# An attention block in split fp32: GpSimd's share of the weight splits in pieces of 256 columns, output weights loaded ahead of y, first key and query tiles in the norm's buffers

## The chip, the cores and the metric

The kernel runs on one core of a Trainium2 chip. The metric is device time in microseconds (us) of one execution, taken as the median of several. The engines are named as the profile names them: PE (TensorE, matrix products and transposes; PEld is its weight load), DVE (VectorE), ACT (ScalarE), POOL (GpSimd) and SP (SyncE, which here issues nearly all DMAs).

## The reference

One layer of a streaming encoder on 1024 tokens of width 1024, all in fp32:

```python
n = rms_norm(h, norm1_g)
qa, ka, va, qb, kb, vb = split(n @ w_in)          # 512,128,128 | 512,512,512 columns
ya = mixer_a(qa, ka, va, sinks)      # window of 3 chunks of 64, 8 heads on 2 key heads, ALiBi, sinks
yb = mixer_b(qb, kb, vb, rel_bias)   # own chunk + 8 before it, 8 heads, relative bias
y = concat(rms_norm(ya, og_a), rms_norm(yb, og_b))
h = h + y @ w_out
u = square(relu(rms_norm(h, norm2_g) @ w_ff1))    # 1024 -> 4096
h = h + u @ w_ff2                                 # 4096 -> 1024
return rms_norm(h, final_norm_g)
```

## The kernel before

**Arithmetic.** Each fp32 operand of a product is held as two rounded parts: hi = round(a) and lo = a - hi. A product is then three matmuls (`mm3`, line 154: hi·hi, hi·lo, lo·hi). So every tile that goes into PE costs an ACT copy (hi, rounded on the way out) and a subtraction (lo). The subtraction is `split_l` (line 133, instruction at L134); the caller says on which engine it runs, DVE or POOL.

**Weights.** `load_weight` (from line 160) takes a staging tile (tag "ws", 3 buffers), loads one weight into it (L110, on SP's queue), has ACT copy hi into one page (L171) and `low_engine` subtract lo into another. A weight of the input projection is a tile of 128 partitions by 8 blocks of 128 columns (1024 columns); a weight of the output projection (`out_weight`) is 128x1024, done in two halves of 512. For the first key and query weights `low_engine` is DVE; for all others here it is POOL. The weights of the MLP have a split of their own that the change does not touch.

**Projection.** `project` computes 512 tokens of 128 projected columns in one PSUM tile. `place` takes it out: DVE multiplies by the tokens' scale R (L242 for q, L244 for k) into a tile `ts_...` (tag "tst", 2 buffers), ACT copies hi, POOL or DVE subtracts lo, and DMAs of SP spread the parts over the K and Q tiles that the attention reads (L251 for Q, L254 for K). A v tile is kept and transposed on PE later (`turn_v`, VA and VvB in the profile). The "tst" buffer is free again when those DMAs have landed.

**Stages.** (1) Start: x and its transpose are loaded; kA, qA0 and vA are projected for both halves t of the tokens (`first_place`), and the norm's scales are computed. The tiles of x wait in "xs" (6 buffers of the pool `sp`, released as a whole before the attention begins). (2) Mixers A and B, 42 to about 407 us: units of attention (scores S, exponentials P, normalisation L494 or L559, transposes pt, products av), interleaved on PE with "filler" work: the other input projections (qA1 to qA3, then kB, qB, vB four times) and the first half of the output projection (`out_proj_a`: weights o0 to o3, and the rows y of mixer A, which had been written to DRAM as yd and are loaded again by `load_y`, L633). (3) The second half of the output projection, the MLP in a form with seven products instead of eight, and the last norm.

**What sets the order.** Each engine works its instructions off in order. PE's order is written out by hand: with `pe_order` on, each PE instruction depends on the one before. The other engines' orders come from a scheduler, which goes by the order in the source and by dependencies. `load` (from line 108) adds a dependency on the marked load before it (`last_load`), which keeps SP's loads behind that one. All DMAs of SP go through one queue in the order of SP; an issue that has to wait holds back all behind it. Both kernels have the same PE instructions in the same order.

Of the kernel before, what the change touches and what calls it, by code (L numbers as in the profile page):

```python
# [9 lines left out]
F32R = mybir.dt.float32r  # L10
# [5 lines left out]
P = 128  # L16
# [4 lines left out]
HALF = 512  # L21
DFF = 4096
NQ = DFF // (4 * P)
HD = 64
# [2 lines left out]
BIG = 3e38  # L27
QA0, KA0, VA0, QB0, KB0, VB0 = 0, 512, 640, 768, 1280, 1792
NPAGES = 35
GQ = 2  # L30
AHEAD1 = 2
AT_ONCE = 3
# [12 lines left out]
def kernel(  # L45
# [34 lines left out]
    def f(ap):  # L80
        return ap.bitcast(F32)
# [51 lines left out]
    def split_l(engine, lo, full, hi):  # L133
        engine.tensor_tensor(lo, full, f(hi), ALU.subtract)  # L134
# [25 lines left out]
    def load_weight(src, shape, name, low_engine, cuts=1, pieces=1):  # L160

        st = stage(shape, f"st_{name}")
        w = [page(shape, f"w{hl}_{name}") for hl in range(2)]

        def steps():
            n = shape[1] // cuts
            for i in range(0, shape[1], n):
                load(st[:, i : i + n], src[:, i : i + n])
                for j in range(i, i + n, n // pieces):
                    c = slice(j, j + n // pieces)  # L170
                    nc.scalar.activation(w[0][:, c], st[:, c], AF.Copy)  # L171
                    split_l(low_engine, w[1][:, c], st[:, c], w[0][:, c])
                yield

        if cuts > 1:
            return w, steps()
        for _ in steps():
            pass
        return w
# [18 lines left out]
    xs = {}  # L198
# [30 lines left out]
            n = [nT[t][hl][k // 2][:, k % 2, :] for hl in range(2)]  # L229
            mm3(acc, (w[0][:, k], w[1][:, k]), n, k == 0, k == NK - 1)  # L230

    def place(acc, kind, name, dst, t, low_engine):
        if name == "vA":
            st = page([P, 2, HALF], f"ts_{name}_{t}")
        else:
            st = main.tile([P, 2, HALF], F32R, tag="tst", bufs=2, name=f"ts_{name}_{t}")
        c = slice(t * HALF, (t + 1) * HALF)
        if kind == "v":
            nc.vector.tensor_tensor(f(st[:, 0]), acc, R1[:, c], ALU.mult)
            return lambda *where: turn_v(st, name, dst, t, *where)  # L240
        if kind[0] == "q":
            nc.vector.scalar_tensor_tensor(f(st[:, 1]), acc, HD**-0.5, R1[:, c], ALU.mult, ALU.mult)  # L242
        else:
            nc.vector.tensor_tensor(f(st[:, 1]), acc, R1[:, c], ALU.mult)  # L244
        nc.scalar.activation(st[:, 0], f(st[:, 1]), AF.Copy)
        split_l(low_engine, st[:, 1], f(st[:, 1]), st[:, 0])
        for hl in range(2):
            for s in range(2):
                src = f(st[s * HD : (s + 1) * HD, hl])
                if kind == "q":  # L250
                    nc.sync.dma_start(f(dst[s][hl * HD : (hl + 1) * HD, c]), src)  # L251
                else:
                    for rep in range(2):
                        nc.sync.dma_start(f(dst[2 * hl + s][rep * HD : (rep + 1) * HD, c]), src)  # L254

    def turn_v(st, name, dst, t, psum, tag, bufs):
        tp = psum.tile([P, 4, 2, HD], F32, tag=tag, bufs=bufs, name=f"vt_{name}_{t}")
# [19 lines left out]
    def in_proj(c0, kind, name, dst, new):  # L277

        w = proj_weight(c0, name, nc.gpsimd)
        yield  # L280
        later = None
        for t in range(2):
            acc = aps.tile([P, HALF], F32, tag="w", bufs=3, name=f"ip_{name}_{t}")
            for k in range(NK):
                project(acc, w, t, (k,))
                if k == 2 and later:
                    later(aps, "w", 3)
                if k == NK - 1:
                    if t == 0:
                        dst.extend(new(name))  # L290
                    later = place(acc, kind, name, dst, t, nc.gpsimd)
                yield
        if later:
            yield
            yield
            later(aps, "w", 3)
# [26 lines left out]

    def first_place(n, t, acc):
        kind, _, name, dst = first[n]
        return place(acc, kind, name, dst, t, nc.vector)

    accs = [first_acc(n, 0) for n in range(3)]
    for n, ks in [(n, (k, k + 1)) for k in range(0, NK, 2) for n in range(2)] + [(2, range(NK))]:
# [7 lines left out]
    Qs = [Q, [], [], []]  # L337
    ahead_A1 = in_proj(QA0 + P, "q", "qA1", Qs[1], new_q)
    next(ahead_A1)
    project(accs[2], wts[2], 1, (0, 1))  # L340
    turns[2](sps, "r", 2)
    project(accs[2], wts[2], 1, (2, 3))
# [287 lines left out]
    def load_y(m):  # L630
        y = new_y(m)
        for t in range(2):
            nc.sync.dma_start(f(y[t]), yd[m, :, t])  # L633
        return y
# [57 lines left out]
    def out_proj_a():  # L692
        ys, ws = [], []
        for m in range(4):
            ys.append(load_y(m))
            ws.append(out_weight(m))
        yield
        for tb in range(TB):
            h = hres[tb] = page([P, D], f"h{tb}", F32)
            nc.sync.dma_start(h, x[tb * P : (tb + 1) * P, :])  # L700
            for dh in range(2):
                c = slice(dh * HALF, (dh + 1) * HALF)
                ps = aps.tile([P, HALF], F32, tag="w", bufs=3, name=f"op_A_{tb}_{dh}")
                for q in range(4):
                    out_proj_step(ps, ys, ws, q, tb, c)
                    if q == 3:
                        nc.vector.scalar_tensor_tensor(h[:, c], ps, rA[:, tb : tb + 1], h[:, c], ALU.mult, ALU.add)  # L707
                    yield
# [537 lines left out]
```

## Time and profile before

| quantity | value |
|---|---|
| runs | 1086.87, 1089.08, 1090.6 us; median 1089.08 |
| profiled execution | 1091.92 us, of it 1090.1 us span (1.8 outside) |
| PE busy in the span | 1056.1 us, 97% |
| DVE, ACT, POOL busy | 759.1 (70%), 535.8 (49%), 426.1 (39%) us |
| mean granted PE clock | 0.994 |
| DMA share of the queue q1 | 47.2% |

A row of the timeline reads: start, duration, engine, line, operation, output <- inputs, shape, count, and in square brackets how long the engine stood idle before it and what released it; where a row holds several instructions, its duration is from the first's start to the last's end. The chain of waits gives per pair of waiting and releasing instruction the total, the count and the longest. A window gives each engine's busy time in a stretch, then the granted PE clock (1.00 is full), the DMA share and the traffic.

### The profile page before, as it was taken

The page shows a single profiled execution, that of the slowest core. Times are in us where ns is not written, and L with a number is a line of the kernel's source. Part 1 is how long each engine was busy: PE and PEld are TensorE (multiplying, and loading weights), DVE is VectorE, ACT ScalarE, POOL GpSimd, SP SyncE. Part 2 cuts the span into 40 slices and gives each one's busy share as a digit, 9 for nine tenths or more (in the row PEclk, how much of TensorE's full clock was granted, in tenths as well). Part 3 has the DMA queues.
Part 4 walks back from the last instruction along what each step waited for, and adds up shares of the span by engine and source line. Part 5 has one row for each costly group of instructions (what it writes and reads, how often), then busy time and mean ns, then how long its engine had stood idle before and what let it go on. Part 6 is the DMA issues. An engine that isn't in the chain of part 4 may idle for free.

```text
span 1090.1 us, 14323 instructions
## 1 busy us (share of the span) xinstructions
PE 1056.1 (97%) x5040; PEld 876.2 (80%) x5040; DVE 759.1 (70%) x1162; ACT 535.8 (49%) x953; POOL 426.1 (39%) x256
## 2 busy tenths in 40 slices
PE   8998999999999999998999999999999999999997
PEld 6787877888878888876888888888788888888885
DVE  5576788757667665597756555655988776778667
ACT  7676766656565466655333333334423333333346
POOL 1364665333252142347644453464014124024125
PEclk9999999999999999998999999999999999999999
DMA  9944626343566432122445255326898545532004
GB/s 332 246 124 120 163 79 170 99 120 113 134 211 239 136 126 107 78 96 95 176 160 188 97 174 174 138 94 248 286 394 316 164 136 173 175 116 97 1 1 155
DMA packets 90584, 170.30 MB, mean 156 GB/s; under 512 B 7824, under 2 KB 43664, under 8 KB 90512
## 3 DMA queue, kind: packets, MB, share of 16 engines
q1 hardware_dynamic: 90368, 169.38, 47.2%
q8 instruction: 40, 0.66, 0.3%
q14 instruction: 32, 0.26, 0.1%
q10 hardware_dynamic: 144, 0.00, 0.0%
HBM read 105.39 MB, written 45.09 MB: 138 GB/s over the span
## 4 chain that ended last, share of the span: by engine, by line
PE 82%; DVE 8%; DMA 3%; ACT 3%; issue 2%; SPq 1%; POOL 1%; DVEq 0%; ACTq 0%
PE f L128 24%; PE f_a L128 16%; PE f_c L128 8%; PE op_B L128 4%; PE f_b L128 4%; PE ip_kB L128 4%; PE op_A L128 4%; PE ip_qB L128 3%; PE ip_vB L128 3%; PE av_B L128 3%; PE ip_qA L128 2%; PE S_B L128 2%; PE pt_B L131 2%; PE S_A L128 1%; PE av_A L128 1%
## 5 line engine op out<-in xcount | busy, mean ns | idle before, releaser
L128 PE MATMUL f<-X,W 128*128 128x512 f32 x1344 | 309.4, 392 | 6.5 <-POOL W L134 5.2
L128 PEld LDWEIGHTS f<-X,W 128*128 128x128 f32 x1344 | 253.6, 189 | 61.3 <-POOL W L134 6.1
L128 PE MATMUL f_a<-V,U 128*128 128x512 f32 x768 | 176.3, 389 | 0.7 <-DVE k L965 0.7
L134 POOL TENSOR_TENSOR U<-u,U 128x1024 fp32r<-128x1024 f32 x32 | 81.7, 2554 | 227.4 <-PE f_c L128 136.3
L128 PEld LDWEIGHTS f_a<-V,U 128*128 128x128 f32 x768 | 144.1, 188 | 31.0 <-issue 1.0
L134 POOL TENSOR_TENSOR W<-T,W 128x1024 fp32r<-128x1024 f32 x32 | 91.5, 2864 | 126.7 <-ACT W L912 126.7
L128 PE MATMUL f_c<-V,U 128*128 128x512 f32 x384 | 88.4, 389 | 0.0
L128 PEld LDWEIGHTS f_c<-V,U 128*128 128x128 f32 x384 | 72.1, 188 | 15.0
L912 ACT ACTIVATE V<-Z 128x1024 fp32r<-128x1024 f32 x32 | 33.9, 1060 | 94.6 <-PE f_a L128 44.6
L134 POOL TENSOR_TENSOR W<-w,W 128x1024 fp32r<-128x1024 f32 x24 | 60.1, 2505 | 36.7 <-ACT W L912 35.1
L134 DVE TENSOR_TENSOR V<-w,V 128x1024 fp32r<-128x1024 f32 x24 | 47.4, 1975 | 29.6 <-ACT V L912 29.6
L912 ACT ACTIVATE U<-u 128x1024 fp32r<-128x1024 f32 x56 | 58.5, 1045 | 13.5 <-DMA ud<-k 7.3
L912 ACT ACTIVATE V<-w 128x1024 fp32r<-128x1024 f32 x24 | 25.4, 1060 | 80.1 <-issue 34.2
L912 ACT ACTIVATE W<-T 128x1024 fp32r<-128x1024 f32 x32 | 33.9, 1059 | 55.0 <-PE f L128 27.7
L955 ACT ACTIVATE k<-f 128x1024 f32<-128x1024 f32 x24 | 24.6, 1026 | 65.8 <-PE f L128 65.8
L390 ACT ACTIVATE P_B<-P_B,nm_B 128x640 f32<-128x640 f32 (+2 forms) x64 | 44.4, 694 | 25.6 <-DVE nm_B L389 13.2
L128 PE MATMUL ip_kB<-nT,w_kB 128*128 128x512 f32 x192 | 52.3, 402 | 3.1 <-DVE ts_qA L242 2.3
L128 PE MATMUL op_A<-w_o,y 128*128 128x512 f32 x192 | 52.1, 397 | 0.2 <-DVE h L707 0.2
L128 PE MATMUL ip_vB<-nT,w_vB 128*128 128x512 f32 x192 | 51.9, 398 | 0.0
L128 PE MATMUL ip_qA<-nT,w_qA 128*128 128x512 f32 x192 | 50.6, 402 | 0.9 <-DVE ts_qA L242 0.9
L128 PE MATMUL ip_qB<-nT,w_qB 128*128 128x512 f32 x192 | 51.5, 396 | 0.0
L134 DVE TENSOR_TENSOR V<-Z,V 128x1024 fp32r<-128x1024 f32 x32 | 45.1, 1412 | 7.1 <-ACT V L912 5.9
(211 smaller groups left out, 2017.7 us busy)
## 6 DMA issues: line engine op xcount, KB each, us to landing
w<-in_w_ff_dram SPq DMA_DIRECT2D x64, 512.0 KB, 4.6
u<-ud SPq DMA_DIRECT2D x56, 512.0 KB, 4.5
ud<-k SPq DMA_DIRECT2D x48, 512.0 KB, 3.0
KkB<-ts_kB SPq DMA_DIRECT2D x64, 128.0 KB, 2.3
yd<-y SPq DMA_DIRECT2D x14, 512.0 KB, 2.8
y<-yd SPq DMA_DIRECT2D x14, 512.0 KB, 6.9
xs<-in_xT_dram SPq DMA_DIRECT2D x16, 256.0 KB, 5.1
xr<-in_x_dram SPq DMA_DIRECT2D x8, 512.0 KB, 7.3
```

The lines of the kernel that those rows point to most:

```text
L128: pe(nc.tensor.matmul(*args, **kw))
L131: pe(nc.tensor.transpose(*args))
L134: engine.tensor_tensor(lo, full, f(hi), ALU.subtract)
L390: nc.scalar.activation(pr[:, :n], pr[:, :n], AF.Exp, bias=nm, scale=-1.0, accum_out=sm)
L912: nc.scalar.activation(w[0], full, AF.Copy)
L955: nc.scalar.activation(kept[p], ps, AF.Copy)
```

## The change

Three edits. **First**, `load_weight` cuts its subtraction into pieces of at most 256 columns when it runs on POOL: a 128x1024 one becomes four, a 128x512 one two. This touches 16 weights of the input projection (vA, qA1 to qA3 and four each of qB, kB and vB) and the two halves of each output weight, o0 to o7. **Second**, the key and query tiles of the first token half (ts_kA_0, ts_qA0_0) are taken from "xs" instead of "tst", and the last DMA that `place` issues for qA0 becomes the mark behind which the following weight loads stand. **Third**, `out_proj_a` asks for the output weights first and for y afterwards.

```diff
+LOW_COLS = 256
...
                     nc.scalar.activation(w[0][:, c], st[:, c], AF.Copy)
-                    split_l(low_engine, w[1][:, c], st[:, c], w[0][:, c])
+                    width = shape[2] if len(shape) > 2 else 1
+                    short = min(n // pieces, LOW_COLS // width) if low_engine is nc.gpsimd else n // pieces
+                    for k in range(j, j + n // pieces, short):
+                        c = slice(k, k + short)
+                        split_l(low_engine, w[1][:, c], st[:, c], w[0][:, c])
...
-    def place(acc, kind, name, dst, t, low_engine):
-        if name == "vA":
+    def place(acc, kind, name, dst, t, low_engine, st=None):
+        if st is not None:
+            pass
+        elif name == "vA":
...
-                    nc.sync.dma_start(f(dst[s][hl * HD : (hl + 1) * HD, c]), src)
+                    last = nc.sync.dma_start(f(dst[s][hl * HD : (hl + 1) * HD, c]), src)
...
+        return last.ins.name
...
     def first_place(n, t, acc):
         kind, _, name, dst = first[n]
-        return place(acc, kind, name, dst, t, nc.vector)
+        st = sp.tile([P, 2, HALF], F32R, tag="xs", bufs=6, name=f"ts_{name}_{t}") if kind != "v" and t == 0 else None
+        return place(acc, kind, name, dst, t, nc.vector, st)
...
     next(ahead_A1)
+    last_load[0] = turns[1]
...
         for m in range(4):
-            ys.append(load_y(m))
             ws.append(out_weight(m))
+            if m > 1:
+                ys += [load_y(2 * m - 4), load_y(2 * m - 3)]
```

What this moves, at three places. SP's queue at the start, where the loads of the weights of qA1 to qA3 (st_qA) meet the DMAs that spread the first keys and queries (KA, QA). Before:

```order
L110 DMA ogc<-in_og_dram 128x8
L110 DMA st_qA_471<-in_w_in_dram 128x8x128
L110 DMA st_qA_572<-in_w_in_dram 128x8x128
L110 DMA st_qA_747<-in_w_in_dram 128x8x128
L254 DMA KA_171<-ts_kA_407 64x512 x2
```

The same queue after:

```order
L111 DMA ogc<-in_og_dram 128x8
L111 DMA st_qA_474<-in_w_in_dram 128x8x128
L261 DMA KA_171<-ts_kA_410 64x512 x2
L261 DMA KA_172<-ts_kA_410 64x512 x2
L261 DMA KA_173<-ts_kA_410 64x512 x2
L261 DMA KA_174<-ts_kA_410 64x512 x2
L258 DMA QA_177<-ts_qA_0_422 64x512
L258 DMA QA_178<-ts_qA_0_422 64x512
L258 DMA QA_177<-ts_qA_0_422 64x512
L258 DMA QA_178<-ts_qA_0_422 64x512
L111 DMA st_qA_578<-in_w_in_dram 128x8x128
L111 DMA st_qA_756<-in_w_in_dram 128x8x128
```

The eight key DMAs and the four query DMAs now stand behind one weight load instead of three.

POOL at the weight of the first query projection of mixer B (w_qB), near which DVE normalises the tile P_A of mixer A; L494 on POOL are POOL's own two of the four normalisations of that unit. Before:

```order
L134 TENSOR_TENSOR ts_qA_0_1052<-ts_qA_0_1052 128x512
L134 TENSOR_TENSOR w_qB_1179<-st_qB_1177,w_qB_1178 128x1024
L494 TENSOR_SCALAR P_A_4_0_1082<-P_A_4_0_1082,rc_A_4_1080 128x256
L494 TENSOR_SCALAR P_A_4_1_1100<-P_A_4_1_1100,rc_A_4_1080 128x256
L134 TENSOR_TENSOR ts_qA_1_1148<-ts_qA_1_1148 128x512
```

And after:

```order
L135 TENSOR_TENSOR ts_qA_0_1067<-ts_qA_0_1067 128x512
L135 TENSOR_TENSOR w_qB_1194<-st_qB_1192,w_qB_1193 128x256
L505 TENSOR_SCALAR P_A_4_0_1097<-P_A_4_0_1097,rc_A_4_1095 128x256
L505 TENSOR_SCALAR P_A_4_1_1115<-P_A_4_1_1115,rc_A_4_1095 128x256
L135 TENSOR_TENSOR w_qB_1194<-st_qB_1192,w_qB_1193 128x256 x3
L135 TENSOR_TENSOR ts_qA_1_1163<-ts_qA_1_1163 128x512
```

One piece now stands ahead of POOL's two normalisations, and three behind them; at the other weights the pieces stand together, where the whole stood.

SP's queue at the output weights of `out_proj_a`, seen at the fourth of them (st_o3), among the reloads of y (y0_0 to y1_3) and the DMAs of a query tile (QqB); names with numbers. Before:

```order
L633 DMA y0_0_3543<-yd_86 128x1024
L454 DMA yd_86<-y1_5_3441 128x1024
L633 DMA y1_0_3544<-yd_86 128x1024
L251 DMA QqB30_3423<-ts_qB3_1_3535 64x512
L251 DMA QqB31_3424<-ts_qB3_1_3535 64x512
L633 DMA y0_1_3555<-yd_86 128x1024
L633 DMA y1_1_3556<-yd_86 128x1024
L110 DMA st_o3_3583<-in_w_out_dram 128x1024
L633 DMA y0_2_3567<-yd_86 128x1024
L633 DMA y1_2_3568<-yd_86 128x1024
```

And after:

```order
L465 DMA yd_86<-y1_5_3489 128x1024
L258 DMA QqB30_3471<-ts_qB3_1_3583 64x512
L258 DMA QqB31_3472<-ts_qB3_1_3583 64x512
L644 DMA y0_0_3621<-yd_86 128x1024
L111 DMA st_o3_3629<-in_w_out_dram 128x1024
L644 DMA y1_0_3622<-yd_86 128x1024
L644 DMA y0_1_3625<-yd_86 128x1024
L644 DMA y1_1_3626<-yd_86 128x1024
L111 DMA st_o4_4541<-in_w_out_dram 128x1024
```

One reload of y now stands ahead of the fourth output weight instead of four; the other reloads follow it. On ACT, the copy of that weight's hi part (w0_o3) moves up past one exponential (P_B4_1_3) and one padding copy; the evacuation of the value tile (VvB30) follows. Before:

```order
L390 ACTIVATE P_B4_1_2_3676,sm_B4_1_3634<-P_B4_1_2_3676,nm_B4_1_3633 128x640
L397 ACTIVATE padL1_546<-pt_B5_0_3_3702 128x128
L390 ACTIVATE P_B4_1_3_3686,sm_B4_1_3634<-P_B4_1_3_3686,nm_B4_1_3633 128x640
L171 ACTIVATE w0_o3_3584<-st_o3_3583 128x512 x2
L261 ACTIVATE VvB30_3662<-vt_vB3_0_3711 128x8x64
```

And after:

```order
L401 ACTIVATE P_B4_1_2_3732,sm_B4_1_3690<-P_B4_1_2_3732,nm_B4_1_3689 128x640
L172 ACTIVATE w0_o3_3630<-st_o3_3629 128x512 x2
L408 ACTIVATE padL1_552<-pt_B5_0_3_3758 128x128
L401 ACTIVATE P_B4_1_3_3742,sm_B4_1_3690<-P_B4_1_3_3742,nm_B4_1_3689 128x640
L269 ACTIVATE VvB30_3718<-vt_vB3_0_3767 128x8x64
```

The copy still stands ahead of the evacuation of the value tile, and now also ahead of the fourth exponential of its unit.

More of the change, by code (lines that the diff above doesn't have):

```diff
@@ L250, in place @@
                 if kind == "q":
-                    nc.sync.dma_start(f(dst[s][hl * HD : (hl + 1) * HD, c]), src)
+                    last = nc.sync.dma_start(f(dst[s][hl * HD : (hl + 1) * HD, c]), src)
                 else:
                     for rep in range(2):
-                        nc.sync.dma_start(f(dst[2 * hl + s][rep * HD : (rep + 1) * HD, c]), src)
+                        last = nc.sync.dma_start(f(dst[2 * hl + s][rep * HD : (rep + 1) * HD, c]), src)
+        return last.ins.name
     def turn_v(st, name, dst, t, psum, tag, bufs):
@@ L291, in in_proj @@
                     later = place(acc, kind, name, dst, t, nc.gpsimd)
+                    later = later if kind == "v" else None
                 yield
```

## The prediction

> **What bounds the kernel now.** I read first the page's line of busy times, then the chain of waits on PE, then windows by stage.
>
> ```profile
> PE 1056.1 (97%) x5040; PEld 876.2 (80%) x5040; DVE 759.1 (70%) x1162; ACT 535.8 (49%) x953; POOL 426.1 (39%) x256
> ```
>
> PE is the bound: it is busy for 1056.1 of 1090.1 us, and its instructions and their order are the same in both kernels. The change can only give back time in which PE stands idle or runs at a lower clock: 34 us of idle in all. What of it lies where the change acts, the chain of waits on PE tells (total us, count, longest):
>
> ```profile
> PE pt_B L131 <- DMA y<-yd: 2.4, 1, 2.4
> PE ip_kB L128 <- DVE ts_qA L242: 2.3, 1, 2.3
> PE S_A L128 <- DVE nm_A L389: 1.3, 1, 1.3
> ...
> PE ip_qA L128 <- DVE ts_qA L242: 0.9, 1, 0.9
> ...
> PE vt_vB L131 <- DVE T_A L134: 0.8, 1, 0.8
> ```
>
> Two windows show the attention stage as a whole and the stretch behind the second of these waits:
>
> ```profile
> 42.40:407.00 364.60, 351.60 (x1926) 296.13 (x1925) 263.38 (x688) 227.18 (x558) 162.78 (x139) 1.00 0.49 143
> 97.10:100.50 3.40, 1.10 (x6) 0.85 (x5) 3.37 (x4) 0.91 (x2) 3.40 (x3) 1.00 0.01 2
> 100.50:103.90 3.40, 3.40 (x13) 3.02 (x13) 2.09 (x9) 1.14 (x5) 1.33 (x3) 0.51 0.62 151
> ```
>
> In the attention PE is busy for 351.6 of 364.6 us, DVE for 263 (72%), POOL for 163 (45%). POOL has room; DVE has some. After the wait at 97 us the clock is 0.51 for 3.4 us.
>
> **A, keys and queries at the start.** SP's queue and its answer on DVE and PE:
>
> ```profile
> 28.77 10.45 DMA st_qA<-in_w_in_dram
> ...
> 32.88 6.82 SPq L254 DMA_DIRECT2D KA<-ts_kA  x8
> ...
> 39.80 2.47 SPq L251 DMA_DIRECT2D QA<-ts_qA  x4
> 41.78 0.69 DVE L244 TENSOR_TENSOR ts_kA<-ip_kA,R 128x512 f32<-128x512 f32 x1 [2.03 <-DMA KA<-ts_kA]
> ...
> 43.42 0.70 PE L128 MATMUL S_A<-KA,QA 128*128 128x256 f32 x4 [0.45 <-issue]
> ...
> 44.99 2.31 PE L128 MATMUL ip_qA<-nT,w_qA 128*128 128x512 f32 x9 [0.86 <-DVE ts_qA L242]
> ```
>
> The key tile was finished at about 30, but its DMAs stand in the queue until 32.88 behind weight loads, one of which takes 10.45 us to land (28.77 to 39.22); the last query DMA is issued at 42.3. With the "tst" buffers held until then, DVE waits 2.03 us to take out the second half, and PE waits 0.45 and 0.86. After the change the twelve DMAs follow one weight load and DVE writes into other buffers: they should be issued from 30 to some 39, with landing before PE is there at 42.97 (43.42 less 0.45). I credit both: **1.3**. Bounds: 0, if the eight key DMAs are themselves the slow part (6.82 us for their issue), to 1.3. The weight loads that now come later, of qA2 and qA3, feed projections that start tens of us on; qA2's split stands at 56.21 (below). They cost nothing unless they are over 10 us late.
>
> **B, the pieces.** Three of the waits come from one pattern, seen in the timeline. At 60, at 99 and at 148 us:
>
> ```profile
> 56.21 2.39 POOL L134 TENSOR_TENSOR w_qA<-st_qA,w_qA 128x1024 fp32r<-128x1024 f32 x1 [1.24 <-issue]
> ...
> 56.90 2.33 DVE L494 TENSOR_SCALAR P_A<-P_A,rc_A 128x256 f32<-128x256 f32 x2
> ...
> 60.09 0.74 PE L128 MATMUL S_A<-KA,QA 128*128 128x256 f32 x4 [1.32 <-DVE nm_A L389]
> ...
> 96.15 2.72 DVE L494 TENSOR_SCALAR P_A<-P_A,rc_A 128x256 f32<-128x256 f32 x2
> 96.23 2.49 POOL L134 TENSOR_TENSOR w_qB<-st_qB,w_qB 128x1024 fp32r<-128x1024 f32 x1 [4.79 <-DVE rc_A L491]
> ...
> 98.79 0.68 DVE L242 SCALAR_TENSOR_TENSOR ts_qA<-ip_qA,R 128x512 f32<-128x512 f32 x1
> ...
> 99.52 2.06 PE L128 MATMUL ip_kB<-nT,w_kB 128*128 128x512 f32 x6 [2.30 <-DVE ts_qA L242]
> ...
> 144.24 2.40 POOL L134 TENSOR_TENSOR w_kB<-st_kB,w_kB 128x1024 fp32r<-128x1024 f32 x1
> 145.05 2.12 DVE L494 TENSOR_SCALAR P_A<-P_A,rc_A 128x128 f32<-128x128 f32 x2
> ...
> 148.40 0.66 PE L131 MATMUL vt_vB<-ident,ts_vB 128*128 128x128 f32 x4 [0.77 <-DVE T_A L134]
> ...
> 292.37 2.39 POOL L134 TENSOR_TENSOR w_vB<-st_vB,w_vB 128x1024 fp32r<-128x1024 f32 x1 [0.81 <-PE av_B L128]
> 292.41 2.56 DVE L559 TENSOR_SCALAR P_B<-P_B,rc_B 128x384 f32<-128x384 f32 x1
> ...
> 295.50 0.33 PE L131 MATMUL pt_B<-ident,P_B 128*128 128x128 f32 x1 [0.47 <-DVE T_B L134]
> ```
>
> DVE's normalisation of an SBUF tile, when it meets POOL's subtraction, ends with it: 56.90 + 2.33 = 59.23 beside POOL's 58.60, 98.87 beside 98.72, 147.17 beside 146.64, 294.97 beside 294.76. Alone the pair is short:
>
> ```profile
> 86.67 0.84 DVE L494 TENSOR_SCALAR P_A<-P_A,rc_A 128x256 f32<-128x256 f32 x2
> ...
> 312.94 2.55 POOL L134 TENSOR_TENSOR w_o<-st_o,w_o 128x512 fp32r<-128x512 f32 x2 [0.76 <-ACT w_o L171]
> ...
> 64.55 1.87 POOL L494 TENSOR_SCALAR P_A<-P_A,rc_A 128x256 f32<-128x256 f32 x2
> ```
>
> So DVE waits for the whole instruction of POOL, up to 2.4 us, and what follows on DVE waits with it. The price of a piece: 1024 columns take 2.39 (the row at 56.21) and 512 take 2.55 / 2 = 1.27, so 512 columns more cost 1.12, the fixed part is 0.15, and 256 columns are an estimated 0.56 + 0.15 = 0.71. Four are 2.84, 0.45 more per weight, on an engine 45% busy. Bounds for a piece: 0.6 (a quarter of 2.39) and 0.93, POOL's one-input operation on 256 columns (1.87 / 2), the nearer in shape but another operation; I take 0.71, by the same operation.
>
> How the waits shrink if DVE gets in after at most one piece:
> - At 60.09, PE waits 1.32 after DVE came 0.69 into the split. With a lock of 0.71, DVE loses at most that instead of 2.33 - 0.84 = 1.49: 0.8 saved (bounds 0.2, where it waits again for a second piece, and 1.3).
> - At 99.52 the order puts one piece ahead of POOL's own normalisations, which wait for the same reciprocal as DVE's. DVE's pair would end near 97.4 instead of 98.87: 1.45 saved of 2.30. The idle stretch is then under 1 us, and the 3.4 us at 0.51, worth 3.4 x 0.49 = **1.7**, go as well.
> - At 148.40: DVE came 0.81 into the split and waited 1.3; 0.6 of PE's 0.77 saved (0.3 to 0.77).
> - At 295.50: DVE waited nearly the whole 2.39; PE's 0.47 is gone.
>
> Sum for B: 0.8 + 1.45 + 1.7 + 0.6 + 0.5 = **5.0**, of it 3.3 without the clock. Other meetings of the two engines ended in no wait of PE, and save nothing.
>
> A rule on the clock speaks against the 1.7. The Trainium skill ("TensorE: Matmul & The Clock Gate", Part 1) says the clock halves after at least one idle window of about 3.4 us. By it a gap of 2.3 us would never have cost a half-clock stretch, and the sum would be 1.7 lower. The rows at 99.52 and 100.50 disagree: 2.30 us idle, within a window PE filled to 1.10 of 3.40, and 0.51 behind it. I go by the rows.
>
> **C, output weights ahead of y.** The wait of 2.4 is put down to y's reload, but PE's transpose needs no y. What its timeline shows:
>
> ```profile
> 316.59 0.39 SPq L110 DMA_DIRECT2D st_o<-in_w_out_dram  x1
> 317.06 3.69 SPq L633 DMA_DIRECT2D y<-yd  x4
> ...
> 324.75 1.15 ACT L171 ACTIVATE w_o<-st_o 128x512 fp32r<-128x512 f32 x2 [2.29 <-PE ip_vB L128]
> 325.81 0.58 ACT L261 ACTIVATE VvB<-vt_vB 128x512 fp32r<-128x512 f32 x1
> 326.42 0.69 DVE L134 TENSOR_TENSOR VvB<-vt_vB,VvB 128x512 fp32r<-128x512 f32 x1 [2.40 <-ACT VvB L261]
> 327.17 0.44 PE L131 MATMUL pt_B<-ident,P_B 128*128 128x128 f32 x2 [2.41 <-DMA y<-yd]
> ```
>
> The fourth weight is issued at 316.59, amid reloads of y; ACT stands still 2.29 us for it, then evacuates the value tile (325.81), DVE subtracts (326.42), and only then is PE's PSUM buffer free. If ACT had not waited, its evacuation would have been done 2.3 us sooner. After the change the weight follows one reload instead of four. It is issued when its staging buffer is free: POOL is through with the first output weight at 312.94 + 2.55 = 315.5 at present, a little sooner with ACT's copy moved up; call it 315. Median landing times of DMAs of this size over the whole program, and of the output weights in the stretch from 308 to 330 us:
>
> ```profile
> yd<-y SPq DMA_DIRECT2D x14, 512.0 KB, 2.8
> y<-yd SPq DMA_DIRECT2D x14, 512.0 KB, 6.9
> ...
> st_o<-in_w_out_dram SPq DMA_DIRECT2D x4, 512.0 KB, 8.8
> ```
>
> By 2.8 or 6.9 it lands at 317.8 or 321.9, before ACT comes to it (324.75 less 2.29: 322.5); by 8.8 at 323.8, with 1.3 of the wait left. With three of the four reloads gone from ahead of it I take the former, and credit **2.4**. The other bound: in the new order ACT's copy is ahead of the last exponential of its unit. A landing past 324, delayed by the reloads that follow, would hold that exponential too: 1.15 for the copies and some 0.2 more, -1.3. All of y's reloads move back; the products that read them come after the weights' splits, and POOL's last ends at 324 or later, so they have that cover; without it up to the landing time of 6.9 us would be exposed once.
>
> **Sum.** On the profiled execution (1091.92, span 1090.1): 1.3 + 5.0 + 2.4 = 8.7, a span of 1081.4. The median shown is 1089.08, 2.8 below that execution, with runs 3.7 apart, so some of what this profile lost to the clock is not in each run; I give the clock term by half against the median: 1089.08 - 7.9 = **1081.2**.
>
> **Rivals.**
> 1. *DVE pays a piece each time.* Its two normalisations may each meet a new piece, since POOL's pieces stand back to back: then 2 x 0.7 of 2.33 remain, and the waits at 60 and 148 stay largely. B is then 0.2 + 1.45 + 0 to 1.7 + 0.3 + 0.2, so 2.2 to 3.9, and with A and C whole 5.9 to 7.6: 1081.5 to 1083.2. For it: DVE's ends lie right behind POOL's ends in all four rows. Against: at 99 the order leaves only one piece ahead. The Trainium skill ("SBUF — State Buffer", section on the two separate sides) has an exclusive lock held for a whole instruction by whichever starts first; by that rule DVE enters after one piece, POOL's next piece then waits for DVE, and each further operation of DVE may wait for one piece more. The rows agree on the whole instruction; none shows what follows between pieces.
> 2. *The fourth output weight is still late.* C is 0 to -1.3; with A and B, and half the clock term, 5.4 to 4.1 are left: 1083.7 to 1085. For it: the median of 8.8 at this very place.
> 3. *No difference:* removed waits come back at the next late item. DVE is at 72%, and behind each wait it had used PE's stall to catch up; if two thirds or more of the 7.0 without the clock come back elsewhere, 2.3 or less is left: 1086.8 to 1089.
> 4. *Slower:* pieces dearer than thought. If a piece costs 1.0 or more (POOL's 0.93 on 256 columns is near it) every one of the 16 input weights takes 1.6 us longer, arrives later at its projection, and meets more of DVE's operations. It decides from the point at which each such weight adds a wait of 0.7 us on PE: 16 x 0.7 = 11.2, less A and C, 3.7: +7.5, 1096.6. Against: POOL is 45% busy, and stood idle for 4.79 us before the split at 96.23.
>
> **How the numbers follow.** 0.3% (3.3 us, about what a measurement of this kernel can tell from no change) sets the line at 1085.8 and 1092.4. The forecast as summed has 0.48. Rivals 1 and 2 have 0.17 and 0.13, all in "faster". Rival 3 has 0.17, rival 4 0.05. So faster 0.78, same 0.17, slower 0.05. Range: down by the upper bounds of B (0.5 + 0.2 more, and the other 0.85 of the 2.30), by the clock's other half (0.85) and by another stretch of 1.7 that may fall away by shifts, to 1077.0; up through rivals 1 and 2 and the near part of 3 to 1086.5.
>
> **What would show it.** Right: POOL's pieces at 0.65 to 0.8; no DVE row of a normalisation pair over 1.6; PE waits at ip_kB under 1 and a full clock behind it; no wait of ACT for the fourth output weight and none of PE's transpose behind it; KA and QA issued before 39. Wrong: pieces over 0.9; DVE pairs still at 2.3; a new PE wait of over 1 us for a weight's split, or for y at the first product of the output projection; the span outside 1077 to 1087.

## The result and the profile after

The changed kernel takes **1081.9 us** (median of 4 runs, 1080.06 to 1082.73), the kernel before 1089.84 (4 runs beside them, 1086.87 to 1092.43). The ratio is 0.9926, with a 95% interval from 0.9896 to 0.9955: 8 us faster, between 5 and 11. The profiled execution has a span of 1081.0 us against 1090.1. The forecast was 1081.2, and 8.7 us on the profiled execution; 9.1 came.

The page's line of busy times and three rows of the list of waits on PE (lines are counted one or a dozen higher in the changed kernel):

```profile
PE 1051.4 (97%) x5040; PEld 873.0 (81%) x5040; DVE 754.9 (70%) x1162; ACT 535.9 (50%) x953; POOL 436.7 (40%) x320
...
PE S_A L129 <- DVE nm_A L400: 2.6, 2, 2.0
...
PE ip_kB L129 <- DVE ts_qA L249: 0.7, 1, 0.7
...
PE pt_B L132 <- DVE T_B L135: 0.2, 1, 0.2
```

The wait of 2.3 at ip_kB is now 0.7, the one of 2.4 put down to y is gone, and so is that of 0.9 at ip_qA. POOL works 10.6 us more. But the score products S_A wait 2.6 instead of 1.3: something took the place of what went.

Where each microsecond went can be read off because PE does the same 5040 instructions in the same order in both. I take one instruction, find it in both timelines and subtract the starts; where that lead grows, time was won. The profiles of the kernels shown here differ by up to 1.5 us in when PE is through with the first projections; 0.3 us of this lead is there already at 42.6 us, ahead of the waits that A is about.

| PE instruction | before | after | lead | step |
|---|---|---|---|---|
| first S_A | 43.42 | 42.49 | 0.93 | A |
| ip_qA behind it | 44.99 | 42.96 | 2.03 | A |
| second S_A | 47.14 | 47.16 | -0.02 | A given back |
| S_A at 60 | 60.09 | 59.53 | 0.56 | B |
| ip_kB | 99.52 | 97.25 | 2.27 | B |
| ip_kB, some products on | 105.36 | 101.63 | 3.73 | B, clock |
| vt_vB | 148.40 | 143.74 | 4.66 | B |
| pt_B | 295.50 | 289.69 | 5.81 | B |
| pt_B | 327.17 | 318.74 | 8.43 | C |
| f of the MLP | 506.53 | 497.13 | 9.40 | neither |

**B** shows in the timeline at the places that the prediction named: POOL's pieces, DVE's normalisation pair beside them, and PE.

```profile
56.34 2.92 POOL L135 TENSOR_TENSOR w_qA<-st_qA,w_qA 128x256 fp32r<-128x256 f32 x4 [1.27 <-issue]
...
57.04 1.64 DVE L505 TENSOR_SCALAR P_A<-P_A,rc_A 128x256 f32<-128x256 f32 x2
...
59.53 0.74 PE L129 MATMUL S_A<-KA,QA 128*128 128x256 f32 x4 [0.61 <-DVE nm_A L400]
...
95.50 1.09 DVE L505 TENSOR_SCALAR P_A<-P_A,rc_A 128x256 f32<-128x256 f32 x2
95.55 0.89 POOL L135 TENSOR_TENSOR w_qB<-st_qB,w_qB 128x256 fp32r<-128x256 f32 x1 [4.76 <-DVE rc_A L502]
...
97.25 0.96 PE L129 MATMUL ip_kB<-nT,w_kB 128*128 128x512 f32 x3 [0.71 <-DVE ts_qA L249]
...
141.12 1.40 DVE L505 TENSOR_SCALAR P_A<-P_A,rc_A 128x128 f32<-128x128 f32 x2
...
287.22 0.92 DVE L570 TENSOR_SCALAR P_B<-P_B,rc_B 128x384 f32<-128x384 f32 x1
```

DVE's 2.33, 2.72, 2.12 and 2.56 have become 1.64, 1.09, 1.40 and 0.92. Four pieces take 2.92 where DVE meets them. The windows of the attention and of the stretch at 97 us, and a later one in the MLP (columns: stretch, length, busy time of PE, PEld, DVE, ACT, POOL, then the PE clock, DMA share, GB/s):

```profile
42.40:407.00 364.60, 357.26 (x1964) 301.73 (x1963) 257.84 (x689) 230.84 (x564) 174.83 (x199) 1.00 0.50 148
...
97.10:100.50 3.40, 3.25 (x18) 2.81 (x19) 3.11 (x11) 1.73 (x5) 3.40 (x6) 1.00 0.41 89
493.30:496.70 3.40, 3.40 (x10) 2.66 (x9) 3.40 (x3) 1.06 (x1) 3.40 (x2) 0.50 0.52 151
```

PE is busy 3.25 of 3.40 us where it was 1.10, and no halved clock follows. In the MLP one window of 3.4 us at half the clock is left of two (before, 6.83 us from 499.93 on): that is the last step of the table, at a place which no edit touches.

**C**, the fourth output weight (SP's issue, ACT's copy, the value tile, PE):

```profile
309.21 0.37 SPq L111 DMA_DIRECT2D st_o<-in_w_out_dram  x1
...
314.65 1.15 ACT L172 ACTIVATE w_o<-st_o 128x512 fp32r<-128x512 f32 x2 [1.18 <-DMA st_o<-in_w_out_dram]
...
316.98 0.60 ACT L269 ACTIVATE VvB<-vt_vB 128x512 fp32r<-128x512 f32 x1 [0.20 <-PE ip_vB L129]
...
317.83 0.68 DVE L135 TENSOR_TENSOR VvB<-vt_vB,VvB 128x512 fp32r<-128x512 f32 x1
...
318.74 0.38 PE L132 MATMUL pt_B<-ident,P_B 128*128 128x128 f32 x2
```

ACT still waits 1.18 us for the weight, but early: its next work, the value tile, comes when PE's product is ready, and PE doesn't wait.

**A** is what failed. SP's queue, POOL's first bias, DVE's first score reduction, PE's second S_A; the first two rows are of before, the others of the changed kernel:

```profile
42.31 1.07 SPq L418 DMA_DIRECT2D b_A<-in_dist_dram  x2
...
44.78 2.16 POOL L419 TENSOR_SCALAR b_A<-b_A 128x256 f32<-128x256 f32 x2 [6.72 <-DVE ts_kA L134]
...
29.90 6.41 SPq L261 DMA_DIRECT2D KA<-ts_kA  x8
...
36.41 2.47 SPq L258 DMA_DIRECT2D QA<-ts_qA  x4
...
38.92 1.31 SPq L111 DMA_DIRECT2D st_qA<-in_w_in_dram  x2
...
40.27 1.63 SPq L429 DMA_DIRECT2D b_A<-in_dist_dram  x2
...
45.45 1.67 POOL L430 TENSOR_SCALAR b_A<-b_A 128x256 f32<-128x256 f32 x2 [4.89 <-issue]
46.34 0.35 DVE L400 CUSTOM_DVE_ANT_0 P_A<-S_A,b_A,nsink 128x128 f32<-128x128 f32 x1 [2.36 <-POOL b_A L430]
...
47.16 0.74 PE L129 MATMUL S_A<-KA,QA 128*128 128x256 f32 x4 [1.97 <-DVE nm_A L400]
```

Keys and queries go out from 29.90 and are all issued by 38.88, as foreseen, and the waits of 0.45 and 0.86 are gone. But the two weight loads that were moved now stand right ahead of the two bias loads b_A. Before, POOL had the bias 2.47 us after its DMA was issued (42.31 to 44.78); now it takes 5.18 (40.27 to 45.45). DVE needs the bias for the first scores, and PE's next scores wait for DVE: 2 us won, 2 us given back.

### The profile page after: what moved, and what is told of

Same layout as the page of the kernel before. It is cut to its first block, busy times and chain, and to the rows that moved or that the text cites. A ratio compares the mean times of both kernels' runs of the same rounds, so it can differ in the third digit from the quotient of the medians.

```text
span 1081.0 us, 14384 instructions
## 1 busy us (share of the span) xinstructions
PE 1051.4 (97%) x5040; PEld 873.0 (81%) x5040; DVE 754.9 (70%) x1162; ACT 535.9 (50%) x953; POOL 436.7 (40%) x320
## 4 chain that ended last, share of the span: by engine, by line
PE 85%; DVE 7%; ACT 3%; issue 2%; DMA 2%; POOL 1%; SPq 1%; DVEq 0%; ACTq 0%
PE f L129 24%; PE f_a L129 16%; PE f_c L129 8%; PE op_B L129 4%; PE f_b L129 4%; PE op_A L129 4%; PE ip_qB L129 4%; PE ip_vB L129 3%; PE ip_kB L129 3%; PE av_B L129 3%; PE ip_qA L129 3%; PE S_B L129 2%; PE pt_B L132 2%; PE S_A L129 1%; PE av_A L129 1%
## 5 line engine op out<-in xcount | busy, mean ns | idle before, releaser
L135 DVE TENSOR_TENSOR V<-w,V 128x1024 fp32r<-128x1024 f32 x24 | 52.0, 2166 | 30.7 <-ACT V L924 30.2
L135 DVE TENSOR_TENSOR T_B<-pt_B,T_B 128x512 fp32r<-128x512 f32 (+2 forms) x72 | 39.7, 552 | 16.7 <-ACT T_B L408 16.3
```

## The experiments

The account to be tested: the pieces end a lock between GpSimd and DVE, the output weights end the late value tile, and the key and query edit is eaten up by the bias. Times are medians; ratios, and gains against before, are against the kernel before run beside each, with 95% intervals. That kernel took 1089.84 us beside the changed one and 1089.63 to 1091.44 beside the others, so a difference of medians between two of the variants is uncertain by over 1 us; where it matters, the difference by the ratios stands with it.

**Each edit alone.** First the pieces (the change's hunk in `load_weight`, nothing else):

```diff
+                    short = min(n // pieces, LOW_COLS // width) if low_engine is nc.gpsimd else n // pieces
+                    for k in range(j, j + n // pieces, short):
```

> The kernel before with the first edit alone (pieces of 256 columns on GpSimd). Theory 1 (the lock): the changed kernel gained 5.8 us of lead on PE between 47 and 300 us, all by this edit, so this kernel gains 5 to 6.5 us against before, its normalisation pairs on DVE at 60, 99, 148 and 295 us take 0.9 to 1.7 us, the 2.4 us wait near 327 us stays, and the first waits near 43 us (0.45 and 0.86) stay. Rival (shift): the pieces only matter because the start and the output weights were moved too; then this kernel gains less than 3 us and some DVE pairs are still above 2 us.

Measured: 1086.4 us, ratio 0.9964 (0.9952 to 0.9977): 3.9 us, between the rival's figure (under 3) and theory 1's 5 to 6.5. By the profile the lead is 5.8 at 295 us, as expected; then part of it is lost again at the fourth output weight, issued in the first of these rows:

```profile
309.92 0.42 SPq L111 DMA_DIRECT2D st_o<-in_w_out_dram  x1
...
319.36 1.15 ACT L172 ACTIVATE w_o<-st_o 128x512 fp32r<-128x512 f32 x2 [3.31 <-DMA st_o<-in_w_out_dram]
...
321.77 0.48 PE L132 MATMUL pt_B<-ident,P_B 128*128 128x128 f32 x1 [2.91 <-DVE VvB L135]
```

The weight is copied 9.4 us after its issue, before 8.2 (316.59 to 324.75): PE waits 2.91 instead of 2.41, here put down to the value tile (VvB), and two windows at half the clock followed in this execution. Theory 1 on the lock holds, its sum for the whole didn't.

Second, the key and query edit:

```diff
+        st = sp.tile([P, 2, HALF], F32R, tag="xs", bufs=6, name=f"ts_{name}_{t}") if kind != "v" and t == 0 else None
...
+    last_load[0] = turns[1]
```

> The kernel before with the second edit alone (first key and query tiles in the norm's buffers, weight loads behind their DMAs). Theory 1: nothing is gained, because the bias loads of mixer A, which now stand behind two weight loads, land no sooner than before (45.4 against 44.8 us) and the second score product waits for them: 0 us, between -0.7 and +0.7, with a new PE wait of 1.5 to 2.1 us at the second S_A. Rival (the forecast): the two waits of 0.45 and 0.86 go and nothing takes their place: 1.3 us faster.

Measured: 1090.5, ratio 0.9998 (0.9985 to 1.001). No gain can be told, as theory 1 has it, and the bias is late here too:

```profile
39.36 1.56 SPq L424 DMA_DIRECT2D b_A<-in_dist_dram  x2
...
44.47 1.67 POOL L425 TENSOR_SCALAR b_A<-b_A 128x256 f32<-128x256 f32 x2 [5.26 <-issue]
...
46.18 0.74 PE L128 MATMUL S_A<-KA,QA 128*128 128x256 f32 x4 [2.11 <-DVE nm_A L395]
```

A window at half the clock followed this wait (from 47.08). The late bias is the rule: in all seven profiles of kernels that have it behind two weight loads, POOL starts on it 5.05 to 5.36 us after its issue; in the other seven, 2.36 to 2.55. What it costs varies more: the second S_A starts at 45.87 to 47.16 in those seven, 46.4 on average and latest in the changed kernel's, and at 46.23 to 47.14, 46.9 on average, in the four with the start of before. So the edit may be worth half a microsecond, which so few executions can't show.

Third, the output weights:

```diff
         for m in range(4):
-            ys.append(load_y(m))
             ws.append(out_weight(m))
+            if m > 1:
+                ys += [load_y(2 * m - 4), load_y(2 * m - 3)]
```

> The kernel before with the third edit alone (output weights asked for ahead of y). Theory 1: 2.4 to 2.7 us faster, the PE wait at pt_B near 327 us gone, ACT's wait for the fourth output weight under 1.3 us, and the 2.3 us gap at 99.5 us still there. The half-clock stretch behind that gap is there again if it comes with the gap (0.51 over 3.4 us), and is gone if it was chance. Rival (the POOL pieces of the output weights are needed as well, since the staging buffer comes free after GpSimd's subtraction of the first one): 0 to 1 us.

Measured: 1088.46, ratio 0.9979 (0.9966 to 0.9992): 2.3 us by the ratio and 1.7 by the medians, near theory 1's 2.4 to 2.7, with no wait near 327 us. The gap of the whole weight split is there, and so is the halved clock behind it:

```profile
99.29:102.70 3.41, 0.76 (x4) 0.61 (x4) 3.38 (x5) 0.87 (x2) 3.27 (x3) 1.00 0.01 2
102.70:106.11 3.41, 3.41 (x14) 3.01 (x13) 1.81 (x7) 1.09 (x4) 1.28 (x1) 0.50 0.52 130
```

**First and third together**, without the key and query edit (both diffs above):

> The first and third edits together, without the second (the changed kernel with its first keys and queries placed as before). Alone, the pieces gave 3.9 us and the output weights 2.3, the key and query edit nothing, and with all three 8 us: 1.8 are missing. Theory 1 (the pieces and the output weights need each other: with pieces alone the fourth output weight came later still, PE waited 2.9 us for it and two half-clock windows followed): this kernel is within 0.8 us of the changed one, 7.2 to 8.8 faster than before, with no wait at pt_B near 320 us. Rival (the key and query edit matters in company): it is 1.5 to 2.5 us slower than the changed kernel.

Measured: 1083.41, ratio 0.9941 (0.9927 to 0.9955), 6.4 us: nearly the sum of 3.9 and 2.3. The wait at pt_B near 320 us is gone, as theory 1 has it. But by the medians it is 1.5 slower than the changed kernel, the rival's lower figure, and 1.7 slower than the kernel with the output weights' halves whole (1081.71, below), which ran beside it and has the key and query edit. Its profiled span, 1080.5, is no longer than the changed kernel's 1081.0; in this execution, though, PE came to the second S_A 0.9 us sooner than in that of before, with the same order at the start. From there to 506 us both gain alike, 9.5 and 9.4. So the first and third edits make the whole gain behind the start; whether the second is worth 1 to 2 us in company stays open. Alone it is worth nothing that can be measured.

**The bias loads ahead of the moved weight loads**, in the changed kernel:

```diff
-                    nc.sync.dma_start(far, dist)
+                    ins = nc.sync.dma_start(far, dist)
+                    if self.j == 0:
+                        last_load[0] = ins.ins.name
```

> The changed kernel with the two bias loads of mixer A ahead of the second and third query weights' loads. Theory 1: the bias lands at 41 to 43 us instead of 45.4, GpSimd has the first bias ready by 44, the wait of 2.0 us at the second S_A falls under 0.5, and the kernel is 1.5 to 2.0 us faster than the changed one (about 9.5 to 10.5 faster than before). Rival: the next late item is just behind (the exponentials' table load on ACT, the second half's key DMAs): the wait moves to one of the next score products, and under 0.7 us is gained.

Measured: 1081.2, ratio 0.9913 (0.9899 to 0.9927): 0.7 faster than the changed kernel by the medians, 1.4 by the ratios, which decides for neither. The profile confirms the cause of the new wait, and speaks for the rival:

```profile
39.17 1.07 SPq L429 DMA_DIRECT2D b_A<-in_dist_dram  x2
...
41.61 1.67 POOL L432 TENSOR_SCALAR b_A<-b_A 128x256 f32<-128x256 f32 x2 [0.85 <-DVE ts_kA L251]
...
44.94 0.64 PE L129 MATMUL S_A<-KA,QA 128*128 128x256 f32 x4
...
59.28 0.74 PE L129 MATMUL S_A<-KA,QA 128*128 128x256 f32 x4 [1.72 <-DVE nm_A L400]
```

POOL has the bias 2.44 us after the issue again, PE's second S_A starts 2.2 us sooner, at 44.94, without a wait. Of the 2.2 us, 0.8 goes at 51 us, where another S_A waits 0.67, and most of the rest at 59.28, where one waits 1.72 (the changed kernel 0.61, at 59.53): 0.25 is left. DVE's normalisation beside the split of the next weight, which comes ahead of these scores, began at 56.79 instead of 57.04: that stretch had hardly moved.

**Size of the pieces.** 512 and 128 columns in place of 256:

```diff
-LOW_COLS = 256
+LOW_COLS = 512
```

> The changed kernel with pieces of 512 columns instead of 256 (two per input weight, output weights as before). Theory 1 (DVE waits for at most the piece that is running, once per operation of its pair): a piece takes 1.27 us, the DVE pairs at 60, 99, 148 and 295 us take 1.3 to 2.1 us, and about half of the 5.8 us stays: 2 to 3.5 us slower than with 256. Rival (only the wait for one whole 1024 is long enough to reach PE): within 0.7 us of 256.

Measured: 1082.48, ratio 0.9921 (0.9899 to 0.9943), 0.6 slower than the changed kernel by the medians and 0.5 faster by the ratios: the rival's figure. But by the starts of PE's instructions its lead over the changed kernel falls by 1.9 us between 47 and 318 us (from +0.90 to -1.01), 1.5 of it up to 295; it is covered by the start, where the bias came 0.9 sooner in this execution, and by some 1.5 in the MLP, where the half-clock window fell ahead of the waits for POOL, which were shorter (4.1 instead of 5.3 in all). Pairs on DVE take 2.05 at 56 us and 1.80 at 141, between the two others:

```profile
56.17 2.05 DVE L505 TENSOR_SCALAR P_A<-P_A,rc_A 128x256 f32<-128x256 f32 x2
...
97.40 1.65 PE L129 MATMUL ip_kB<-nT,w_kB 128*128 128x512 f32 x6 [1.24 <-DVE ts_qA L249]
...
141.40 1.80 DVE L505 TENSOR_SCALAR P_A<-P_A,rc_A 128x128 f32<-128x128 f32 x2
```

Of the 5.8 that 256 columns gave between 47 and 295 us, 512 keep 4.35, three quarters. In this one profile theory 1's direction holds, not its size; the times don't show it.

```diff
-LOW_COLS = 256
+LOW_COLS = 128
```

> The changed kernel with pieces of 128 columns (eight per input weight, four per half of an output weight). From 0.15 us fixed and 1.12 per 512 columns a piece is 0.43, eight 3.4 us, 0.6 more per input weight than with 256. Theory 1: DVE pairs shrink to about 1.2 us, of PE waits little is left to take, so 0 to 1 us faster. Rival (DVE waits for a piece at each of its operations, and more pieces mean more meetings; GpSimd later by 0.6 to 1 us per weight): 0.5 to 3 us slower, with PE waits for the low part of weights.

Measured: 1087.52, ratio 0.9962 (0.9946 to 0.9978): slower than the changed kernel by 5.6 (medians) or 3.9 (ratios), either worse than the rival; its 12 runs spread from 1082.8 to 1090.72. In the profile PE ends 4.7 us behind the changed kernel, and most of that arises beside one row:

```profile
311.56 5.92 POOL L135 TENSOR_TENSOR w_o<-st_o,w_o 128x128 fp32r<-128x128 f32 x14
313.47 4.36 DVE L570 TENSOR_SCALAR P_B<-P_B,rc_B 128x640 f32<-128x640 f32 x1
```

One normalisation on DVE, 0.55 us elsewhere, lasted 4.36 us beside a run of POOL pieces that took 5.92 / 14 = 0.42 each. It was not held by one piece, but by ten in a row, to the run's end at 317.48. Against the changed kernel PE falls behind by 3.5 us at this place, between that kernel's 316 and 319 us, the start of a half-clock window included. Elsewhere the shorter pieces do shorten the waits: no other normalisation on DVE lasts over 0.85 here, against 1.11 in the changed kernel. But in a long run they can leave DVE no turn at all.

**One weight whole.** In the changed kernel only w_qB0's subtraction, at 95 us, is in one instruction again:

```diff
-... if low_engine is nc.gpsimd else n // pieces
+... if low_engine is nc.gpsimd and name != "qB0" else n // pieces
```

> The changed kernel with one weight's subtraction, that of w_qB0 near 96 us, in one instruction again. Theory 1: DVE's pair there takes 2.5 to 2.8 us again instead of 1.09, the wait at ip_kB returns to 2.2 to 2.4 us (0.7 with pieces), and, if the halved clock comes with such a gap, 1.5 us more: 1.6 us slower without a half-clock stretch, 3.2 with. Rival (the waits come back elsewhere, later units catch up): under 0.7 us.

Measured: 1084.4, ratio 0.9934 (0.9911 to 0.9956): slower than the changed kernel by 2.5 (medians) or 0.9 (ratios), so the times alone don't separate theory 1 (1.6 or 3.2) from the rival. The profile does, with the pair and the wait that theory 1 names, at which PE falls 1.6 behind the changed kernel:

```profile
94.91 2.72 DVE L505 TENSOR_SCALAR P_A<-P_A,rc_A 128x256 f32<-128x256 f32 x2
...
98.28 1.65 PE L129 MATMUL ip_kB<-nT,w_kB 128*128 128x512 f32 x6 [2.32 <-DVE ts_qA L249]
```

Its windows, cut as the clock's own would fall (counted in steps of 3.413 us from the half-clock window at 479.34 in this execution):

```profile
93.65:97.06 3.41, 2.31 (x17) 1.83 (x15) 2.81 (x5) 2.13 (x6) 2.10 (x1) 1.00 0.01 2
97.06:100.47 3.41, 2.19 (x11) 1.88 (x12) 3.35 (x9) 1.27 (x4) 3.41 (x4) 1.00 0.12 28
100.47:103.88 3.41, 3.41 (x18) 2.88 (x18) 1.79 (x8) 2.37 (x10) 0.96 (x2) 1.00 0.86 226
```

The same gap of 2.3 us, and no halved clock: here it lay across two windows, idle 1.10 in one and 1.22 in the next. That fits a rule by which the halved clock comes with the gap only if one window gets enough of it (last section).

**Output weights' halves whole**, input weights in pieces:

```diff
-... if low_engine is nc.gpsimd else n // pieces
+... if low_engine is nc.gpsimd and width > 1 else n // pieces
```

> The changed kernel with the output weights' halves subtracted in one instruction of 512 columns each, as before; input weights stay in pieces. Theory 1 (on GpSimd's longest uninterrupted run, 16 pieces in 12.2 us, the pieces do no good: 4 us blocked for one normalisation were seen with 128 columns): within 0.7 us of the changed kernel, with GpSimd done with the first four output weights about 1 us sooner. Rival (there too the length of one instruction is what DVE waits for): its normalisations between 308 and 320 us take up to 1.5 us instead of 0.9, and 0.7 to 2 us are lost.

Measured: 1081.71, ratio 0.9926 (0.9912 to 0.994): as the changed kernel, as theory 1 has it. GpSimd is through with the fourth output weight at 316.56 instead of 318.51, of which PE's lead explains 1.3; DVE's longest normalisation there takes 1.25 instead of 0.92, and no wait of PE follows. For the first four output weights the pieces do nothing. At the next, near 381 us, a normalisation takes 1.35 instead of 1.03, and PE loses 0.4 there; the times don't show it.

**Pieces in the MLP too.** Behind the start, PE's longest waits are now for POOL's splits there (1.85 and 3.40 us). In the changed kernel:

```diff
-        split_l(engine, w[1], full, w[0])
+        if name[0] != "W":
+            split_l(engine, w[1], full, w[0])
+        else:
+            for k in range(4):
+                split_l(engine, w[1][:, k], full[:, k], w[0][:, k])
```

> The changed kernel with GpSimd's 28 splits of the first MLP weight's operands also in four pieces of one 256-column block each. PE waits there for GpSimd's low parts for 1.85 and 3.40 us, and its products need them block by block. Theory 1: the first piece is enough for PE to start, DVE's sums of two SBUF inputs beside them wait less, and 2 to 5 us are gained, the half-clock stretch behind the 3.4 us gap included. Rival (four pieces cost 0.45 more each and the two waits are for GpSimd's queue as a whole): -0.5 to +1.5 us.

Measured: 1077.77, ratio 0.9874 (0.985 to 0.9898): faster than the changed kernel by 4.1 (medians) or 5.7 (ratios), theory 1's figure or more. PE's wait for POOL's W falls from 5.3 to 0.2; two rows of the list of waits show what comes in its place, and three of the timeline why (the last is of the changed kernel):

```profile
PE f L129 <- DVE k L981: 2.2, 1, 2.2
...
PE f L129 <- POOL W L135: 0.2, 1, 0.2
```

```profile
477.07 5.16 POOL L135 TENSOR_TENSOR W<-w,W 128x256 fp32r<-128x256 f32 x4
...
479.26 7.01 DVE L135 TENSOR_TENSOR X<-S,X 128x512 fp32r<-128x512 f32 x7
...
482.58 4.30 DVE L135 TENSOR_TENSOR X<-S,X 128x512 fp32r<-128x512 f32 x7
```

DVE's subtractions of two SBUF tiles took 7.01 us beside the pieces; in the changed kernel the same seven took 4.30, with POOL idle for most of that time (480.4 to 485.3). So DVE doesn't wait less, as theory 1 had it, and the half-clock stretch is still there, at 494.88. PE starts on the first piece and is 5.4 us ahead of the changed kernel at 487 (0.8 of it from the start, where the bias came sooner); then it gives 2.3 back when DVE is late. Another 1.7 comes at 757 and 766 us, at waits for DVE that are shorter; why, the runs don't show.

**The best of both**, and pieces of 512 in the MLP instead (the bias hunk and the MLP hunk together; the second steps by two blocks):

```diff
-            for k in range(4):
-                split_l(engine, w[1][:, k], full[:, k], w[0][:, k])
+            for k in range(0, 4, 2):
+                c = slice(k, k + 2)
+                split_l(engine, w[1][:, c], full[:, c], w[0][:, c])
```

> The changed kernel with the bias loads first and the MLP's splits in four pieces. Theory 1: the pieces in the MLP keep their 4 us, the bias order adds 0 to 1, since most of its 2.1 us is given back at the score products of 51 and 59 us: 4 to 5 us faster than the changed kernel, 12 to 13.5 faster than before. Rival: the bias order adds its full 2.1: 6 us faster than the changed kernel.

Measured with four pieces: 1076.68, ratio 0.9879 (0.9863 to 0.9894): 13 us faster than before, 5.2 faster than the changed kernel by the medians, just above theory 1's 4 to 5. Against the MLP's pieces alone that is 1.1 faster by the medians and 0.5 slower by the ratios, so what the bias order adds is not settled; in its profile an S_A waits 1.9 us at 58 us, and a window at half the clock follows.

> As the run before, with the MLP's splits in two pieces of 512 columns instead of four. In the four-piece kernel DVE's subtractions for X beside GpSimd's run of pieces took 7.0 us instead of 4.3, and PE waited 2.2 us for DVE behind them. Theory 1 (fewer pieces, fewer turns that DVE loses): DVE's run takes 4.5 to 6, that wait shrinks, PE's first product starts one 512-column piece later (0.6 us each at two places): within 1 us of four pieces. Rival (only the wait for the first piece counts): 1 to 2.5 us slower than four pieces.

Measured with two: 1078.16, ratio 0.9895 (0.9876 to 0.9914), 1.5 slower than four, the rival's figure. DVE's run took 6.49 us, more than theory 1's 4.5 to 6, and the wait for DVE stayed at 2.0, so its cure did nothing; that two pieces are worse is not settled, since the six runs spread from 1075.72 to 1081.13, and a wait of 1.8 us at 176 us, which no other of these kernels had, lies in its profile too.

## Why the prediction was right, step by step

The total was right, and partly by luck: of the 8.7 us foreseen on the profiled execution A gave 1.3 less, B and C together 1.0 more, and a window at half the clock that fell away in the MLP gave 1.0 that no edit was to bring; 0.3 went again behind the last products.

- **A, 1.3 foreseen, 0 measured.** The step that failed is the sentence that the weight loads that come later "feed projections that start tens of us on" and so cost nothing. True of the projections; but a moved load also delays what stands behind it in the queue. The two bias loads of mixer A stood there, and PE's second S_A waits, by way of DVE's first reduction, for POOL's work on them. With the bias first the new wait is gone; in that profile the gain is then lost again by 59 us, so even without the bias 1.3 was too much. The row to look at was POOL's b_A at 44.78, two microseconds ahead of PE's second S_A.
- **B, 5.0 foreseen, 5.8 measured** in the table (lead from -0.02 to 5.81). By place: 0.6 at 60 us (0.8 foreseen), 1.7 at 99 (1.45), 1.5 behind it by the clock (1.7), 0.9 up to 148 (0.6), 1.15 up to 295 (0.5; part of it, 0.39 at 247 us, came from a place not named). That DVE waits as long as GpSimd's instruction lasts is shown by putting back one instruction (2.72 on DVE, 2.32 on PE) and by 512 columns (2.05 and 1.80).
- **The price of a piece, 0.71 foreseen.** Where they meet no normalisation of DVE, four take 2.8, 0.70 to 0.71 each; where they do, up to 3.6 (198.62 to 202.21). POOL's busy time grew by 10.6 us; 16 x 0.45 = 7.2 and 16 halves at 0.15 = 2.4 make 9.6 of it.
- **Rival 1 had its share.** DVE's two operations did wait for a piece each, 1.64 and 1.40 in all at 57 and 141 us, not once as I took for 60 us, and 1.64 lies just over the 1.6 that I had named as the limit. It cost 0.2 at 60. With 128 columns the worse form of that rival happened.
- **C, 2.4 foreseen, 2.6 measured** (8.43 - 5.81), 2.3 (0.9 to 3.7) alone. The issue, foreseen at 315 by the time of before, came at 309.21 with PE 5.8 ahead, which is the same. The landing took 5.4 us, between the 2.8 and 6.9 that I went by; ACT's wait did not go, as I had it, but fell to 1.18, and early enough. That the wait named after y was for the weight was only argued ahead; that it goes when y is loaded later and the weight sooner shows it.
- **The clock, 1.7 of the sum, half against the median.** The rule that the trace follows is below; by it a gap of 2.3 us meets a halved clock in an estimated 6 of 10 executions, about 1.0 on average. Giving it by half was near; the reason is the place of the gap in a grid, which the prediction didn't know. By the same rule C's gap had a share too, which I left out, and so has A's new one: in two of the seven profiles with it (the key and query edit alone, and 128 columns) a halved clock followed.

## What to carry to other kernels

When a load is moved back, follow the queue behind its new place to the first one that an idle engine will need, not only the load's own user. In these runs a long GpSimd subtraction held up DVE's normalisations of SBUF tiles to its end (2.72 us for a pair of 0.84), so cutting it paid where the two met and the wait reached the bounding engine; but a long unbroken run of short ones once shut DVE out for 4.36 us, and 256 columns were the best of the three sizes by the profile (512 did as well by the time). Compare two kernels by the starts of the bounding engine's instructions where its order is the same: gains and losses of 1 us that cancel in the total stand out there. Take off first the lead that was there before the change acts, and compare several executions before a step of 1 us is believed.

## What the runs showed of the hardware

**The clock.** In the profiles of all fourteen kernels the granted clock is 1.00 or 0.50, and between the start and the last few us every stretch at 0.50 lasts 3.41 us or twice that. Within a profile their starts lie on a grid of 3.413 us, whose place differs from one execution to the next. I laid that grid over PE's busy time in each profile. All 16 windows there in which PE was idle for more than 1.86 us were followed by one at half the clock; between 1.81 and 1.86 it was 7 of 9; below that one window was, with 1.54 in the kernel with 128 columns, and two that were at half the clock themselves. The two rows of before at 97.10 and 100.50 (1.10 busy) and those of the kernel with one whole weight (idle 1.10 and 1.22, no halving) are the two sides of it. With 1.85 as the limit, a gap of 2.3 us can lie across the grid in such a way that neither window gets 1.85 of it; the share of places at which one does is an estimated (3.41 - 1.85 + 2.3 - 1.85) / 3.41 = 0.59. The Trainium skill ("TensorE: Matmul & The Clock Gate", Part 1) has the same length of window, free-running, and the same two clocks, which these traces bear out; that a whole idle window is needed they do not, since some 54% of one was enough (1.85 of 3.41).

**The lock.** POOL's pieces of 0.42 us followed each other through 4.36 us while one DVE operation waited. At its other meetings with pieces of this size a normalisation on DVE took at most 0.85 us in all. What decides between the two is not settled by these runs.
